# One more attention head turned through VectorE and HBM, two heads a unit sooner, and the last two down-projection units in the other order

## The chip, the cores and the metric

The kernel runs on one NeuronCore of a Trainium2 chip. TensorE (PE in the profile; PEld is its weight load) multiplies, VectorE (DVE), ScalarE (ACT) and GpSimd (POOL) do the elementwise work, and SyncE (SP) issues most of the transfers between HBM and the on-chip memory. Every engine works through its own instructions in the order in which the program issued them, and waits at an instruction until what it needs is there. The metric is the device time of one execution in microseconds (us).

## The reference

One encoder layer over 256 tokens of width 2048, in float32. Cut to what matters:

```python
h = rmsnorm(x); q, k, v, u = split(h @ w_in)        # 12 query heads, 4 key/value heads of 128
scores = q @ k.T * 128**-0.5 + alibi                # window |t - s| <= 128
m = max(scores.max(-1), sink)
p = exp(scores - m); p = p / (p.sum(-1) + exp(sink - m))
a = rmsnorm(p @ v)                                  # 1536 wide
f = rmsnorm(fourier_mix(u))                         # 512 wide
x = x + concat([a, f]) @ w_out
g, val = split(rmsnorm(x) @ w_up)                   # 5504 wide each
x = x + (gelu(conv3(g)) * val) @ w_down
y = rmsnorm(x)
```

## The kernel before

**Precision.** Each float32 operand of a product is split into a rounded part "hi" and a remainder "lo", and three products (hi by hi, hi by lo, lo by hi) are summed in PSUM. For a unit of weights, ACT writes hi (line 194, `split_high`) and DVE writes lo = raw - hi (line 202, `split_low`).

**Units.** All weights come in units of 128 x 2048 floats (1 MB; the last four are 128 x 1536). SP loads a unit into one of three `raw` buffers (line 178). The load of unit i + 3 is issued when unit i has been split, as its buffer is then free. The splits run two units ahead of the products (`step`, `ff_step`), into three buffers each of `hi` and `lo`. Units 0 to 3 make u, 4 to 7 v, 8 to 23 the four keys and twelve queries, 24 to 39 the output projection (`w_out`), and the rest the feed-forward part.

**Work beside the units.** The order of everything is written out by hand. Three tables, `before`, `beside` and `behind`, hold functions under a unit's number. `unit(i, ...)` runs `before[i]`, the unit's matmuls, `beside[i]`, the split of unit i + 2, and `behind[i]`. So what is `beside` unit i stands in the queues of ACT, DVE and SP ahead of the split of unit i + 2.

**A head's way.** The query of head h is slot s of the units (head 9 is 21, head 10 is 22, head 11 is 23), and each step is placed at a unit s + n. The scores are taken before unit s + 2 and leave PSUM beside it (`scores_out`), the exponentials run behind it (`exps`), and beside s + 3 `weigh` divides by the sums (lines 714, 717). The 256 x 256 weights must then be turned, so that the keys lie on the partitions, for the product with v (`values`, line 769). There are two ways:

- Heads 10 and 11 (not in `FLIPS`) are turned on TensorE: four 128 x 128 transposes before unit s + 4 (`turn`, line 724), split out of PSUM beside it (`turn_out`, lines 736 and 737), product before s + 5.
- Heads 0 to 9 (in `FLIPS`) are turned by the others: beside s + 3 DVE transposes 32 x 32 blocks (`flip_out`, line 327) and four transfers write them to HBM (line 330); beside s + 4 one transfer reads them back in the right order (`flip_in`, line 338); beside s + 6 they are split (`flip_parts`, lines 759 and 760); and the product stands before s + 7.

`values_out` (lines 494, 295, 296) leaves the product beside the same unit as a tile `cat`, which units 24 on multiply with `w_out`. The tile of head 10 is first read in unit 29. `total_scale` (lines 505 to 523) takes the sums of squares of the Fourier part behind unit 25.

**The end.** The last four units (`in_w_down_last`, called L0 to L3 here; i is L0's number) are multiplied twice: for the first 128 tokens (b = 0) in the order L0, L1, L2, L3, then for the others (b = 1). Each `last_product(c, b)` is nine matmuls (lines 1336 to 1338), after which DVE adds the result to the residual (line 1181), ACT squares it, and POOL multiplies it by the last norm's factors (line 1176). The splits of L0 and L1 are made two items ahead as before. Then the kernel before splits L3 (unit i + 3, `own_tiles`) into buffers of its own, and after `last_product(0, 0)` it calls `ff_step`, which runs what is left beside that item (the additions of the last `down` item, `down_out`, line 1162) and splits L2.

Of the kernel before, what the change touches and what calls it, by code (L numbers as in the profile page):

```python
# [18 lines left out]
NH = 12  # L19
# [46 lines left out]
for _g in range(NKV):  # L66
    QK_ORDER += [("k", _g)] + [("q", _g * GQA + _i) for _i in range(GQA)]

FLIPS = range(NH - 2)
QK_FIRST = {n: (2, 2) if n in (8, 12) else (1, 0) for n in range(16)}  # L70
N_U, N_V, N_QK = 0, 4, 8
N_OUT = N_QK + len(QK_ORDER)
# [25 lines left out]
def ff_items():  # L98


    def ups(first, end):
        return [(kind, j) for j in range(first, end) for kind in ("gate", "val")]

    firsts = [first for first, _ in GROUPS] + [LATE[0], NF]
    items = ups(0, firsts[1])
    for g, pattern in enumerate(PATTERNS):
        todo = {
            "u": ups(firsts[g + 1], firsts[g + 2]),
            "s": [("product", g, c, p) for c in range(2) for p in PRODUCTS[c]],
            "d": [("down", c) for c in range(4)],  # L110
        }
        items += [todo[c].pop(0) for c in pattern]
        assert not (todo["u"] or todo["s"]), (g, todo)
    return items + [("last", c) for c in range(4)]
# [3 lines left out]
def block_kernel(  # L118
# [27 lines left out]
    def f32(ap):  # L146
        return ap.bitcast(F32)

    def bank(pool, name):
        return pool.tile([P, 512], F32, tag=pool.name, name=name)  # L150
# [6 lines left out]
    items, up_index = ff_items(), {}  # L157
# [16 lines left out]
    def load(i):  # L174
        if i < len(units) and i not in raws:
            src, n = units[i]
            raws[i] = wp.tile([P, 2048], F32, tag="raw", name=f"raw{i}", bufs=RAW)
            nc.sync.dma_start(raws[i][:, 0:n], src)
# [8 lines left out]
    def split_high(i, o=0, n=2048, tiles=parts_of):  # L187

        if i >= len(units):
            return  # L190
        if i not in halves:
            tiles(i)
        s = slice(o, min(o + n, units[i][1]))
        nc.scalar.activation(halves[i][0][:, s], raws[i][:, s], AF.Copy)  # L194

    def split_low(i, o=0, n=2048, reload=True):

        if i >= len(units):
            return
        hi, lo = halves[i]  # L200
        s = slice(o, min(o + n, units[i][1]))
        nc.vector.tensor_tensor(lo[:, s], raws[i][:, s], f32(hi[:, s]), ALU.subtract)  # L202
        if s.stop == units[i][1] and reload:
            load(i + RAW)
            load_more(i + RAW)

    def split(i):

        split_high(i)
        split_low(i)  # L210
# [32 lines left out]
    def u_part(k, o, n, m=1):  # L243

        rows = ux[k // 4][:, (k < 4) * U_HEAD :].rearrange("p (k c) -> p k c", k=4)
        return rows[:, k % 4 : k % 4 + m, o : o + n]
# [22 lines left out]
    def load_more(i):  # L269

        if i == 6:
            nc.sync.dma_start(chan, c_chan)
            nc.sync.dma_start(wfs, wf)
            nc.sync.dma_start(pos, c_pos)
        if i == 7:
            nc.sync.dma_start(vec[:, 0:V_N], vecs)
            nc.sync.dma_start(rel, c_rel)
# [103 lines left out]
    before, beside, behind = {}, {}, {}  # L381

    def at(when, i, f, *a):
        when.setdefault(i, []).append((f, a))

    def run(when, i):
        for f, a in when.pop(i, []):
            f(*a)
# [13 lines left out]
    for k in range(NK):  # L402
# [3 lines left out]
        n = 1 if c < 2 else 2  # L406
# [3 lines left out]
        if q % n == 0:  # L410
            w, h = u_part(k, 0, FW, n), hi[:, q : q + n, :]
# [238 lines left out]
    def qk_out(kind, h, ps):  # L650
        tmp = ph.tile([P, S], F32, tag="tmp", name=f"tmp_{kind}{h}", bufs=2)
        nc.scalar.activation(tmp, ps[:, S : 2 * S], AF.Copy)
        add = ph.tile([P, S], F32, tag="add", name=f"add_{kind}{h}", bufs=2)
        nc.vector.tensor_tensor(add, ps[:, 0:S], tmp, ALU.add)
        if kind == "k":
            nc.vector.tensor_tensor(add, add, r1b, ALU.mult)
        st["add", kind, h] = add
# [120 lines left out]
        feature_out(st.pop(("o", h))[:, 0:S], h, vcol(V_GA + h), sq_a, h == 0)  # L778


    slot_of = {kh: N_QK + n for n, kh in enumerate(QK_ORDER)}
    for i in range(N_QK, N_OUT + 8):
        heads = {i - s: h for (kind, h), s in slot_of.items() if kind == "q"}
        new = [kh for kh, s in slot_of.items() if i - s == 1]
        for n, h in sorted(heads.items()):
            if n == 5 + 2 * (h in FLIPS):
                at(before, i, values, h)
        if 4 in heads and heads[4] not in FLIPS:
            at(before, i, turn, heads[4])
        if 2 in heads:  # L790
            at(before, i, scores, heads[2])
        for kind, h in new:
            at(beside, i, lambda k=kind, h=h: qk_out(k, h, st.pop(("ps", k, h))))
        if 6 in heads and heads[6] in FLIPS:
            at(beside, i, flip_parts, heads[6])
        for kind, h in new:
            at(beside, i, qk_parts, kind, h)
        for n, h in sorted(heads.items()):
            if n == 5 + 2 * (h in FLIPS):
                at(beside, i, values_out, h)  # L800
        if 3 in heads:
            at(beside, i, weigh, heads[3])
            if heads[3] in FLIPS:
                at(beside, i, flip_out, heads[3])
        if 4 in heads:
            at(beside, i, flip_in if heads[4] in FLIPS else turn_out, heads[4])
        if 2 in heads:
            at(beside, i, scores_out, heads[2])
        if 2 in heads:
            at(behind, i, exps, heads[2])  # L810
# [68 lines left out]
    for n, (c, kq) in enumerate(OUT_ORDER):  # L879
        i = N_OUT + n  # L880
# [14 lines left out]
        if kq >= 2:  # L895
            part = "a" if kq == 2 else "f"
            ps = ps_a[c] if kq < 3 else ps_a[c, "f"]
            last = c in added
# [171 lines left out]
    def split_item(n):  # L1070
        if n >= len(items):
            return
        it = items[n]
        if n in up_index:
            split(up_index[n])
            if pending:
                pending.pop(0)()
        else:
            while pending:
                pending.pop(0)()  # L1080
            split_product(*it[1:])

    def ff_step(n):
        run(beside, n)
        split_item(n + 2)
        run(behind, n)
# [91 lines left out]
    def last_post(c, b, ps, o=0, n=512):  # L1178

        xb = xs[c][:, b, o : o + n]  # L1180
        nc.vector.tensor_tensor(xb, ps, xb, ALU.add)
        if o + n < 512 or c < 3:
            k = c if c < 3 else 4
            junk = wp.tile([P, 512], F32, tag="junk", name=f"junkc{c}{b}")
            nc.scalar.activation(
                junk[:, 0:n], xb, AF.Square, scale=D**-0.5, accum_out=ssq3[:, b, k : k + 1]
            )
# [58 lines left out]
    for q in range(OPEN):  # L1246
# [6 lines left out]
        if q == 1:  # L1253
            i = up_index[3]
# [71 lines left out]
    i = up_index[n]  # L1326


    def last_product(c, b, o=0, n=512):
        hi, lo = halves[i + c]  # L1330
        ps = bank(dn, f"ps_e{c}{b}{o}")[:, 0:n]
        for q, k in enumerate(LAST):
            w = slice(q * 512 + o, q * 512 + o + n)
            ah, al = (act[k][:, p * S + b * P : p * S + (b + 1) * P] for p in range(2))
            end = q == len(LAST) - 1
            nc.tensor.matmul(ps, ah, hi[:, w], start=q == 0, stop=False)
            nc.tensor.matmul(ps, al, hi[:, w], start=False, stop=False)
            nc.tensor.matmul(ps, ah, lo[:, w], start=False, stop=end)
        if (c, b) == (0, 0):
            ff_step(items.index(("last", 0)))  # L1340
        last_post(c, b, ps, o, n)

    split_high(i + 3, tiles=own_tiles)
    split_low(i + 3)
    last_product(0, 0)
    first_squares(0)
    by_factors(0, 0, engine=nc.gpsimd)
    for c in (1, 2):
        last_product(c, 0)
        by_factors(c, 0, engine=nc.gpsimd)  # L1350
    last_product(3, 0)
    v = add_squares(0, 0, 512, ssq3[:, 0, 3:4], 4)
    r3 = last_scale(0, other_squares(0, v))
# [128 lines left out]
```

## Time and profile before

| | us |
|---|---|
| median of 3 runs (lowest, highest) | 936.0 (935.55, 936.22) |
| the profiled execution | 935.62 |
| its span, first to last instruction | 933.8 |
| PE busy in the span | 924.0 |
| DVE, ACT, POOL busy | 772.0, 541.9, 62.0 |

The heads 9 to 11 run beside the units 24 to 28, which lie between 155 and 188 us of the span. The first matmul of the last products starts at 908.46 us, the last one at 925.55 us. What follows that is the tail: squares, the last scale, and the transfers out.

How to read it: an answer in order of time has the start in us, the duration in us, the engine, the line of the kernel, the operation, what it writes and what it reads, how many were merged, and in square brackets the idle time of the engine before it and what ended that. Matmuls are pipelined, so each row of PE lasts longer than its distance to the next row's start; that distance (the pitch) is what a matmul costs when nothing waits.

### The profile page before, as it was taken

What the parts mean: (1) busy time and instruction counts of PE and PEld (TensorE: products, weight loads), DVE (VectorE), ACT (ScalarE), POOL (GpSimd) and SP (SyncE); (2) the same over time, 40 slices, a digit from 0 to 9 for tenths busy, and PEclk for the clock granted to TensorE, in tenths of its full rate; (3) what the DMA queues carried; (4) which work ended last, traced back from release to release, by engine and by line L of the source; (5) the groups of instructions that cost most, each with busy time, mean ns of one, the idle gap of its engine ahead of it and who ended that gap; (6) DMA issues with size and microseconds to landing.
All of it is one profiled execution on the core that took longest, in us unless ns stands there. A gap on an engine that the chain in (4) does not pass through costs nothing.

```text
span 933.8 us, 12856 instructions
## 1 busy us (share of the span) xinstructions
PE 924.0 (99%) x4985; PEld 800.2 (86%) x4985; DVE 772.0 (83%) x986; ACT 541.9 (58%) x674; POOL 62.0 (7%) x80
## 2 busy tenths in 40 slices
PE   9999999999999999999999999999999999999996
PEld 7888998888888888888888888888888888888885
DVE  7668988787768877898877997879978789989986
ACT  7756767546455655565555665555655556655553
POOL 0101111200000000000000000000000000000002
PEclk9999999999999999999999999999999999999998
DMA  9965777467677668787798779887787968879652
GB/s 368 312 226 166 241 238 217 175 195 276 223 277 252 202 206 259 241 277 258 232 300 248 246 210 297 221 260 231 274 237 247 299 216 270 248 241 271 188 181 90
DMA packets 57949, 224.44 MB, mean 240 GB/s; under 512 B 23296, under 2 KB 28544, under 8 KB 34336
## 3 DMA queue, kind: packets, MB, share of 16 engines
q1 hardware_dynamic: 53200, 193.86, 57.9%
q0 software_dynamic: 4544, 29.49, 17.1%
q8 instruction: 39, 0.64, 0.3%
q10 hardware_dynamic: 144, 0.26, 0.1%
q14 instruction: 22, 0.18, 0.1%
HBM read 216.78 MB, written 6.82 MB: 239 GB/s over the span
## 4 chain that ended last, share of the span: by engine, by line
PE 96%; DVE 2%; DMA 1%; ACT 1%; issue 1%; POOLq 0%; POOL 0%; ACTq 0%; DVEq 0%
PE ps_val L363 25%; PE ps_gate L363 25%; PE ps_q L363 7%; PE ps_P L1155 3%; PE ps_P L1156 3%; PE ps_P L1157 3%; PE ps_N L1155 3%; PE ps_N L1156 3%; PE ps_N L1157 3%; PE ps_a L348 2%; PE ps_a L346 2%; PE ps_k L363 2%; PE ps_a L347 2%; PE ps_s L675 1%; PE ps_o L769 1%; DVE lo L202 1%
## 5 line engine op out<-in xcount | busy, mean ns | idle before, releaser
L202 DVE TENSOR_TENSOR lo<-raw,hi 128x2048 fp32r<-128x2048 f32 (+2 forms) x133 | 295.1, 2220 | 34.7 <-ACT hi L194 34.3
L194 ACT ACTIVATE hi<-raw 128x2048 fp32r<-128x2048 f32 (+1 forms) x131 | 246.9, 1887 | 29.8 <-PE ps_a L347 11.3
L363 PE MATMUL ps_gate<-hU,hi 128*128 128x512 f32 x688 | 236.1, 389 | 0.0
L363 PE MATMUL ps_val<-hU,hi 128*128 128x512 f32 x688 | 236.1, 389 | 0.0
L363 PE MATMUL ps_gate<-hU,lo 128*128 128x256 f32 x688 | 189.9, 276 | 0.0
L363 PE MATMUL ps_val<-hU,lo 128*128 128x256 f32 x687 | 189.6, 276 | 0.0
L363 PEld LDWEIGHTS ps_val<-hU,hi 128*128 128x128 f32 x688 | 129.1, 188 | 26.9
L363 PEld LDWEIGHTS ps_gate<-hU,hi 128*128 128x128 f32 x688 | 129.1, 188 | 26.8
L363 PEld LDWEIGHTS ps_gate<-hU,lo 128*128 128x128 f32 x688 | 129.1, 188 | 1.3
L363 PEld LDWEIGHTS ps_val<-hU,lo 128*128 128x128 f32 x687 | 128.9, 188 | 1.3
L936 ACT ACTIVATE ft_g<-ps_gate 128x256 f32<-128x256 f32 x43 | 16.5, 384 | 120.6 <-PE ps_gate L363 120.6
L936 ACT ACTIVATE ft_v<-ps_val 128x256 f32<-128x256 f32 x43 | 16.4, 383 | 86.8 <-PE ps_val L363 86.8
L363 PE MATMUL ps_q<-hT,hi 128*128 128x512 f32 x192 | 65.0, 391 | 0.0
L1155 PE MATMUL ps_P<-hi_P,op_P 128*128 128x512 f32 x144 | 56.0, 389 | 0.0
L1156 PE MATMUL ps_P<-hi_P,op_P 128*128 128x512 f32 x144 | 56.0, 389 | 0.0
L1157 PE MATMUL ps_P<-lo_P,op_P 128*128 128x512 f32 x144 | 56.0, 389 | 0.0
L363 PE MATMUL ps_q<-hT,lo 128*128 128x256 f32 x192 | 51.2, 277 | 0.0
L1053 DVE TENSOR_TENSOR lo_N<-sumw,hi_N 128x2048 fp32r<-128x2048 f32 (+1 forms) x20 | 41.5, 2077 | 9.4 <-ACT hi_N L1052 9.2
L1155 PE MATMUL ps_N<-hi_N,op_N 128*128 128x512 f32 x108 | 42.0, 389 | 0.0
L1156 PE MATMUL ps_N<-hi_N,op_N 128*128 128x512 f32 x108 | 42.0, 389 | 0.0
L1157 PE MATMUL ps_N<-lo_N,op_N 128*128 128x512 f32 x108 | 42.0, 389 | 0.0
L363 PEld LDWEIGHTS ps_q<-hT,hi 128*128 128x128 f32 x192 | 35.2, 188 | 6.6
(402 smaller groups left out, 1587.1 us busy)
## 6 DMA issues: line engine op xcount, KB each, us to landing
raw<-in_w_up SPq DMA_DIRECT2D x86, 1024.0 KB, 6.7
raw<-in_w_in SPq DMA_DIRECT2D x20, 1024.0 KB, 5.8
raw<-in_w_out SPq DMA_DIRECT2D x16, 1024.0 KB, 4.8
sumw<-in_w_down POOLq DMA_DIRECT2D x16, 1024.0 KB, 8.6
raw<-in_w_down_late SPq DMA_DIRECT2D x4, 1024.0 KB, 6.9
raw<-in_w_down_last SPq DMA_DIRECT2D x4, 768.0 KB, 4.2
turnp<-flip SPq DMA_DIRECT2D x40, 64.0 KB, 2.2
flop<-turnp SPq DMA_DIRECT2D x10, 256.0 KB, 3.5
```

Of the source, the lines that this page charges most:

```text
L194: nc.scalar.activation(halves[i][0][:, s], raws[i][:, s], AF.Copy)
L202: nc.vector.tensor_tensor(lo[:, s], raws[i][:, s], f32(hi[:, s]), ALU.subtract)
L346: nc.tensor.matmul(ps, ah, wh, start=first and q == q0, stop=False)
L347: nc.tensor.matmul(ps, al, wh, start=False, stop=False)
L348: nc.tensor.matmul(ps, ah, wl, start=False, stop=last and q == q0 + len(kk) - 1)
L363: nc.tensor.matmul(ps[:, x], (hi, lo)[i][:, k * P : (k + 1) * P], hk(k)[:, x], start=n == 0 and k == 0, stop=n == len(order) - 1 and k == ...
L675: nc.tensor.matmul(ps[:, b * S : (b + 1) * S], qT[:, qo + b * P : qo + (b + 1) * P], kT[:, ko : ko + S], start=n == 0, stop=n == 2,)
L936: nc.scalar.activation(tmp, ps[:, S : 2 * S], AF.Copy)
L1053: nc.vector.tensor_tensor(lo, src, f32(hi), ALU.subtract)
L1155: nc.tensor.matmul(ps, o[:, 0, p, :], hi[:, s], start=first and p == 0, stop=False)
L1156: nc.tensor.matmul(ps, o[:, 1, p, :], hi[:, s], start=False, stop=False)
L1157: nc.tensor.matmul(ps, o[:, 0, p, :], lo[:, s], start=False, stop=last and p == n - 1)
```

## The change

Head 10 joins `FLIPS`, so that head 11 alone is turned on TensorE. Heads 9 and 10 are `SOON`: their split and their product stand one unit sooner than for the other flipped heads, at s + 5 and s + 6. For head 9 this is beside unit 26 and before unit 27 (it was 27 and 28). For head 10 it is beside 27 and before 28 (its turn was before 26, and its product before 27). At the end, L2 (i + 2) is split into the buffers of its own ahead of `last_product(0, 0)`, and L3 (i + 3) after it into the common ring, behind the additions of the last `down` item.

```diff
-FLIPS = range(NH - 2)
+FLIPS = range(NH - 1)
+SOON = (NH - 3, NH - 2)
...
+    def values_at(h):
+        return 5 + 2 * (h in FLIPS) - (h in SOON)
+
...
-            if n == 5 + 2 * (h in FLIPS):
+            if n == values_at(h):
                 at(before, i, values, h)
...
-        if 6 in heads and heads[6] in FLIPS:
-            at(beside, i, flip_parts, heads[6])
+        for n, h in sorted(heads.items()):
+            if n == values_at(h) - 1 and h in FLIPS:
+                at(beside, i, flip_parts, h)
...
-            if n == 5 + 2 * (h in FLIPS):
+            if n == values_at(h):
                 at(beside, i, values_out, h)
...
         if (c, b) == (0, 0):
-            ff_step(items.index(("last", 0)))
+            n0 = items.index(("last", 0))
+            run(beside, n0)
+            split(i + 3)
+            run(behind, n0)
         last_post(c, b, ps, o, n)
 
-    split_high(i + 3, tiles=own_tiles)
-    split_low(i + 3)
+    split_high(i + 2, tiles=own_tiles)
+    split_low(i + 2)
     last_product(0, 0)
```

## The prediction

> **What bounds the kernel now.** I read the page first, then PE's waits, then the two places that the diff touches, engine by engine in order of time. The page's rows of busy time and of the chain that ended last:
>
> ```profile
> PE 924.0 (99%) x4985; PEld 800.2 (86%) x4985; DVE 772.0 (83%) x986; ACT 541.9 (58%) x674; POOL 62.0 (7%) x80
> PE 96%; DVE 2%; DMA 1%; ACT 1%; issue 1%; POOLq 0%; POOL 0%; ACTq 0%; DVEq 0%
> ```
>
> In the second row the reader sees that 96% of the chain is TensorE, which the first row has busy for nearly the whole span. So the time can fall only where PE gets fewer instructions, where a wait of PE goes, or in the tail. PE's waits (waited for, us in total, times, longest) show one outside the first units:
>
> ```profile
> PE ps_e L1338 <- DVE lo L202: 0.5, 1, 0.5
> PE ps_u L420 <- ACT hT L295: 0.3, 1, 0.3
> ```
>
> The change touches both kinds: four transposes of PE, and that wait on `lo` in the last products.
>
> **Head 10's transposes go.** PE in order of time about unit 26 (the transposes of head 10 at 168.05) and at the start of unit 27 (the product of head 10, then the transposes of head 11), and the group of all eight transposes (min/median/max ns):
>
> ```profile
> 168.05 0.60 PE L724 MATMUL ps_t<-ident,sc 128*128 128x128 f32 x4
> 168.41 0.48 PE L346 MATMUL ps_a<-hi,cat 128*128 128x512 f32 x1
> 168.72 0.40 PE L347 MATMUL ps_a<-hi,cat 128*128 128x512 f32 x1
> ...
> 174.00 0.40 PE L769 MATMUL ps_o<-pt,v_hi 128*128 128x256 f32 x2
> ...
> 174.71 0.60 PE L724 MATMUL ps_t<-ident,sc 128*128 128x128 f32 x4
> ```
>
> ```profile
> L724 PE MATMUL ps_t<-ident,sc x8: 272/273/276, 168.1 to 175.0; 128*128 128x128 f32 x8
> ```
>
> And PE in the last products, about its wait:
>
> ```profile
> 912.54 0.39 PE L1336 MATMUL ps_e<-hi,act 128*128 128x512 f32 x1
> 912.76 0.39 PE L1337 MATMUL ps_e<-hi,act 128*128 128x512 f32 x1
> 913.64 0.50 PE L1338 MATMUL ps_e<-lo,act 128*128 128x512 f32 x1 [0.49 <-DVE lo L202]
> 913.98 0.40 PE L1336 MATMUL ps_e<-hi,act 128*128 128x512 f32 x1
> ```
>
> The pitch of a 512-wide matmul that waits for nothing is 912.76 - 912.54 = 0.22 by rounded starts; I use 0.23. From the first transpose to the second matmul after it pass 168.72 - 168.05 = 0.67 us. Without transposes it would be one pitch, so they cost 0.67 - 0.23 = **0.44**. Two other values are possible. If the slow first matmul (0.31 to the next) belongs to the change of product and not to the transposes, the gain is 168.41 - 168.05 = 0.36. If each transpose costs its whole duration, it is 4 x 0.273 = 1.09. I take 0.44, as starts on one engine in a stretch without waits leave no room for more; 0.36 and 1.09 stay as ends.
>
> The Trainium skill (TensorE: Matmul & The Clock Gate, Part 4: PE-mode transpose) has about 275 ns for a 128 x 128 transpose in a kernel's context, for bf16, most of it access latency. The row's 273 ns agrees as a duration, but the pitch within this trace is a third of it; by the page's figure as a cost the four would give 1.10 us (an estimate from the page).
>
> The products move without cost: head 9's six matmuls go from unit 28 to 27, head 10's from 27 to 28. PE has as many of them, and each unit as many as before.
>
> **What replaces the transposes.** On ACT and DVE the split from PSUM (lines 736, 737) becomes one in two halves from SBUF, and DVE gets one more block transpose. DVE in order of time, units 24 to 26, and the groups of the flipped tile with the landing of its loads (us, min/median/max):
>
> ```profile
> 156.97 0.71 DVE L327 STREAM_TRANSPOSE flip<-sc 128x512 f32<-128x512 f32 x1
> ...
> 163.28 0.48 DVE L691 CUSTOM_DVE_ANT_0 sc<-ps_s,rel,sink 128x256 f32<-128x256 f32 x1
> ...
> 170.15 1.22 DVE L523 COPY rstdf<-sums_f 32x2 f32<-32x2 f32 x4 [1.79 <-POOL sums_f L519]
> 171.38 0.48 DVE L296 SCALAR_TENSOR_TENSOR cat<-ps_o,vec,cat 128x256 fp32r<-128x256 f32 x1
> 171.78 0.16 DVE L714 RECIPROCAL ex<-sm 128x2 f32<-128x2 f32 x1
> 171.97 0.62 DVE L717 TENSOR_SCALAR sc<-sc,ex 128x256 f32<-128x256 f32 x2
> ```
>
> ```profile
> L760 DVE TENSOR_TENSOR pt<-flop,pt x20: 414/418/973, 97.1 to 175.6; 128x256 fp32r<-128x256 f32 x20
> ...
> DMA to landing us min/median/max: 2.7/3.5/6.4
> ```
>
> Head 10's transpose comes ahead of the row at 163.28 and moves all later work of DVE by 0.71, so the row at 171.38 (head 8's `cat`) could start at 172.09. There now stands head 9's split, moved up one unit: 2 x 0.42 = 0.84, or 0.42 + 0.97 = 1.39 if one half is as slow as the slowest row. It ends at 172.93 (173.48). PE wants it for head 9's product at 174.00 - 0.36 to 0.44, some 173.6: in time by both. Then come head 8's `cat` and head 11's `weigh`, which took 171.97 + 0.62 - 171.38 = 1.21: done at 174.14 (174.69). The transposes of head 11 want that at 174.71 - 0.44 = 174.27. So the spare is 0.13, or PE waits 0.42. This is the tightest place of the change. I take no wait, as 0.42 is the median of twenty halves; 0.42 of waiting stays as an end. `turn_out` of head 10 (line 737) leaves DVE ahead of the split of unit 28, so the work behind is late by about a split less that, and those units are wanted a unit and more later: nothing.
>
> **SP's queue.** SP in order of time: head 9's four writes, the load of unit 29, head 9's read.
>
> ```profile
> 157.71 1.83 SPq L330 DMA_DIRECT2D turnp<-flip  x4
> 160.90 0.35 SPq L178 DMA_DIRECT2D raw<-in_w_out  x1
> 161.93 0.38 SPq L338 DMA_DIRECT2D flop<-turnp  x1
> ```
>
> Five transfers are added. Head 10's writes stand in the queue ahead of head 9's read and wait for the transpose: 163.28 + 0.71 = 163.99. With 1.83 to issue they end at 165.8, and head 9's read moves from 161.93 to about 165.9. It lands after 2.7 to 6.4, median 3.5: at 169.4 (168.6 to 172.3). ACT then needs two halves before DVE can finish, but DVE isn't free before 172.09, so up to a landing near 171 nothing is lost. At 172.3 head 11's `weigh` follows some 0.5 later than worked out, and PE waits up to 0.8. The load of unit 30 behind it waits for DVE's split of unit 27, some 0.71 later, and is used units later. Head 10's read comes when its writes have landed (head 9's were read at 161.93, which is 2.4 after the end of their issues at 157.71 + 1.83 = 159.54), 168.2, and even 6.4 later it is 174.6, ahead of its split beside unit 27 and its product at some 180. Nothing on either.
>
> **The end: L2 before L3.** ACT, then DVE in order of time; then the loads of L1 and L2 (first and last issue, and landing):
>
> ```profile
> 907.44 2.86 ACT L194 ACTIVATE hi<-raw 128x1536 fp32r<-128x1536 f32 x2 [2.96 <-DMA raw<-in_w_down_last]
> ```
>
> ```profile
> 904.51 1.76 DVE L202 TENSOR_TENSOR lo<-raw,hi 128x1536 fp32r<-128x1536 f32 x1 [0.61 <-ACT hi L194]
> 908.97 1.76 DVE L202 TENSOR_TENSOR lo<-raw,hi 128x1536 fp32r<-128x1536 f32 x1 [2.69 <-ACT hi L194]
> 910.64 1.28 DVE L1162 TENSOR_TENSOR xs<-ps_l,xs 128x512 f32<-128x512 f32 x2
> 911.84 1.75 DVE L202 TENSOR_TENSOR lo<-raw,hi 128x1536 fp32r<-128x1536 f32 x1
> ...
> 925.87 0.42 DVE L1181 TENSOR_TENSOR xs<-ps_e,xs 128x256 f32<-128x256 f32 x1 [0.40 <-PE ps_e L1338]
> ```
>
> ```profile
> L178 SPq DMA_DIRECT2D raw<-in_w_down_last x2: 328/328/328, 895.8 to 898.4; - x2
> ...
> DMA to landing us min/median/max: 4.1/4.2/4.2
> ```
>
> This is the wait: ACT stands 2.96 for the load of L3 though L2 has lain there since 898.4 + 4.2 = 902.6. DVE then splits L3 (908.97), does the additions (910.64), and ends L2's `lo` at 913.59; PE has wanted it a pitch after 912.76. After the change L2's `hi` starts when ACT has done L1's (904.5) and takes 2.86 / 2 = 1.43; its `lo` ends near 906.27 + 1.76 = 908.0, 4.5 ahead of need. Gain: 913.98 - 912.76 = 1.22 for two pitches of 0.23, so **0.76**. The row with PE's wait alone gives 0.5, the lower end.
>
> Next in line is L3. Its load has landed by 907.44, where ACT's wait ended, and the ring buffer is free when the last `down` product ends, just after the last products' start. The additions take DVE 1.28 from there (say 908.7 to 910.0), ACT's `hi` runs beside them, and `lo` ends by 911.8. PE comes to L3 after L2's nine matmuls, 912.54 + 9 x 0.23 - 0.44 = 914.2: 2.4 to spare. The tail follows its matmuls: the last addition (925.87) waits for PE, so it moves with PE.
>
> **Sum.** 0.44 + 0.76 = 1.20 off the profiled execution's 935.62: 934.4. That execution stands 0.4 below the median of the runs, 936.0, to which I apply the same: **934.8**, that is 0.13% less. About 0.2% (1.9 us) is what a measurement of this kernel can tell from no change, so my forecast is: the same, on the fast side.
>
> **Rivals.** (1) Slower: head 9's weights come too late, as SP issues head 10's writes first and the read then lands behind them. If the read took its longest, 6.4, only after the writes had landed (2.4), it would come at 165.9 + 8.8 = 174.7. ACT's two halves, DVE's two, `cat` and `weigh` follow: 0.4 + 0.84 + 1.21, and head 11's turn starts at 177.2 and not 174.27: PE waits 2.9. That makes 936.0 - 1.2 + 2.9 = 937.7. It is slower than before from a landing at 173.0 on, 7.1 after the issue, and by more than 0.2% from 174.9 on. Against it: none of the reads in the trace took more than 6.4. (2) The mild form: the read toward its longest, or the slow half: 0.3 to 0.8 of waiting, 935.1 to 935.6. For it speaks the spare of 0.13. (3) Faster by 0.2%: the transposes cost 0.273 each: 1.09 + 0.76 = 1.85, so 934.1, at the edge. Against it: the start at 168.41. (4) The change at the end only moves the wait, to L3: 936.0 - 0.44 = 935.6. Against it: 2.4 to spare.
>
> **How the numbers follow.** My forecast 0.58; (2) 0.20; (3) 0.08, most of it past the bound; (4) 0.04; (1) 0.10, most of it past the bound, since a read that comes so late has no upper end in these rows. So faster 0.07, same 0.85, slower 0.08. The forecast's own range is 934.4 to 935.4: the ends 0.36 and 0.5 give 0.86 instead of 1.20, and the runs spread by some 0.3. For 8 in 10: down to (3)'s 934.1 less 0.1, and up through (2) and (4) to 935.6 and the runs' spread and a second thing of (2)'s size, 936.4.
>
> **What would show it.** Right: no PE wait at line 1338; four rows at line 724 and not eight; unit 26's first matmul right behind head 8's product; the last products beginning 0.44 earlier and the last matmul 1.2. Wrong: a wait of PE at line 769 or 724 near 174 (on `pt` or `sc`), with a read at line 338 that landed after 171; a wait at line 1336 or 1338 for L3's `hi` or `lo`. It would also be wrong if the stretch between, which nothing touches, took another time: its units are fed by the same queues.

## The result

The changed kernel takes 934.57 us (median of 21 runs, 934.04 to 935.96), the kernel before 935.88 (21 runs on the same chips): a ratio of 0.9987, with a 95% interval of 0.9981 to 0.9993. The forecast was 934.8 and 0.13% less. The profiled execution of the changed kernel has 934.68 us and a span of 932.9. Behind the numbers of the experiments stand three runs of 951 to 952 us (one with head 11 flipped too, two of the kernel before), some 15 above all others of their kernel; the medians and ratios leave them out.

PE's waits in the changed kernel (waited for, us in total, times, longest):

```profile
PE ps_warm L289 <- POOL ones L281: 1.0, 1, 1.0
PE ps_u L421 <- ACT hT L296: 0.2, 1, 0.2
```

The wait on `lo` in the last products is gone, and none has come in its place. PE about unit 26, and at the start of unit 27, where the transposes of head 11 are the only ones left:

```profile
168.53 0.28 PE L770 MATMUL ps_o<-pt,v_lo 128*128 128x256 f32 x1
168.65 0.40 PE L347 MATMUL ps_a<-hi,cat 128*128 128x512 f32 x1
168.88 0.40 PE L348 MATMUL ps_a<-hi,cat 128*128 128x512 f32 x1
...
174.73 0.28 PE L770 MATMUL ps_o<-pt,v_lo 128*128 128x256 f32 x1
174.85 0.60 PE L725 MATMUL ps_t<-ident,sc 128*128 128x128 f32 x4
175.21 0.48 PE L347 MATMUL ps_a<-hi,cat 128*128 128x512 f32 x1
```

Unit 26 begins one narrow pitch (0.12) behind head 8's product, and its second matmul follows at 0.23 and not at 0.31: both parts of the 0.44 were the transposes'. At 174.85 head 11's transposes follow head 9's product at the usual pitch, so nothing waited there. DVE shows why that was close (units 25 and 26):

```profile
171.47 1.22 DVE L524 COPY rstdf<-sums_f 32x2 f32<-32x2 f32 x4 [1.79 <-POOL sums_f L520]
172.73 0.76 DVE L761 TENSOR_TENSOR pt<-flop,pt 128x256 fp32r<-128x256 f32 x2
173.41 0.48 DVE L297 SCALAR_TENSOR_TENSOR cat<-ps_o,vec,cat 128x256 fp32r<-128x256 f32 x1
173.80 0.15 DVE L715 RECIPROCAL ex<-sm 128x2 f32<-128x2 f32 x1
173.99 0.62 DVE L718 TENSOR_SCALAR sc<-sc,ex 128x256 f32<-128x256 f32 x2
```

By the last row head 11's weights are done at 174.61, 0.24 ahead of 174.85; the run with a second transpose, below, puts what there was to spare at 0.36. Head 9's read, now behind head 10's writes on SP:

```profile
L339 SPq DMA_DIRECT2D flop<-turnp x1: 399/399/399, 166.7 to 166.7; - x1
...
DMA to landing us min/median/max: 2.8/2.8/2.8
```

It has landed by 169.5, 3 us before DVE is free for it.

The profiled executions of these kernels start differently, by up to 1.2 us in the first units. The comparison by stretches leaves that out: each row is from the start of one first matmul to the start of the next, read from PE in order of time.

| stretch, us | before | changed | difference |
|---|---|---|---|
| start to the first output product (unit 24) | 154.94 | 155.53 | +0.59 |
| that to the first product of unit 28 | 27.14 | 26.69 | -0.45 |
| that to the first up product | 65.33 | 65.33 | 0.00 |
| that to the first of the last products | 661.05 | 661.05 | 0.00 |
| that to the last matmul | 17.09 | 16.31 | -0.78 |
| that to the end | 8.27 | 7.99 | -0.28 |

Two of the three gains were in the prediction with these sizes (0.44 and 0.76). The third, in the tail, was not. The first row is not of the change: over the profiles below it goes from 154.9 to 156.1. In these two profiles most of it lies in the first matmuls of u, where from the first start to the fifth pass 1.11 us before and 1.86 in the changed kernel.

ACT and DVE at the end of the changed kernel:

```profile
903.13 2.87 ACT L195 ACTIVATE hi<-raw 128x1536 fp32r<-128x1536 f32 x2 [3.90 <-PE ps_l L348]
908.57 1.49 ACT L195 ACTIVATE hi<-raw 128x1536 fp32r<-128x1536 f32 x1 [2.57 <-PE ps_l L348]
```

```profile
904.66 3.43 DVE L203 TENSOR_TENSOR lo<-raw,hi 128x1536 fp32r<-128x1536 f32 x2 [0.61 <-ACT hi L195]
908.00 1.49 DVE L1167 TENSOR_TENSOR xs<-ps_l,xs 128x512 f32<-128x512 f32 x2
910.10 1.76 DVE L203 TENSOR_TENSOR lo<-raw,hi 128x1536 fp32r<-128x1536 f32 x1 [0.61 <-ACT hi L195]
```

L1 and L2 are split back to back, done at 908.1, and L3 at 911.9. ACT no longer waits for a load, but for PE to leave the ring buffer.

### The profile page after: what moved, and what is told of

Its sections match the earlier page's. It is cut to its first block, busy times and chain, and to the rows that moved or that the text cites. A ratio compares the mean times of both kernels' runs of the same rounds, so it can differ in the third digit from the quotient of the medians.

```text
span 932.9 us, 12860 instructions
## 1 busy us (share of the span) xinstructions
PE 924.0 (99%) x4981; PEld 800.8 (86%) x4981; DVE 772.4 (83%) x988; ACT 542.3 (58%) x675; POOL 63.0 (7%) x80
## 3 DMA queue, kind: packets, MB, share of 16 engines
q0 software_dynamic: 4544, 29.49, 17.1%
## 4 chain that ended last, share of the span: by engine, by line
PE 98%; DMA 0%; ACT 0%; DVE 0%; issue 0%; POOLq 0%; POOL 0%; ACTq 0%
PE ps_val L364 25%; PE ps_gate L364 25%; PE ps_q L364 7%; PE ps_P L1161 3%; PE ps_P L1160 3%; PE ps_P L1162 3%; PE ps_N L1160 3%; PE ps_N L1161 3%; PE ps_N L1162 3%; PE ps_a L347 2%; PE ps_k L364 2%; PE ps_a L349 2%; PE ps_a L348 2%; PE ps_s L676 1%; PE ps_o L770 1%; PE ps_ff L347 1%
```

## The experiments

All ratios are to the kernel before on the same chip. Their intervals are about 0.0009 to either side, which is 0.8 us: the measured time alone can't tell parts of 0.3 us apart, so the verdicts on the parts rest on the stretches, and the measured time is given beside them. The changed kernel itself was run beside the last group alone.

**The order of the last units alone.** Heads as before:

```diff
-FLIPS = range(NH - 1)
-SOON = (NH - 3, NH - 2)
+FLIPS = range(NH - 2)
+SOON = ()
```

> The order of the last two units alone; heads 9 and 10 as before. Theory (two gains that add: the transposes' pitch on TensorE, 0.44 us, and the wait on lo in the last products, 0.76 us): 0.76 less than before, a ratio of 0.9992, no wait of PE at the lo matmul of the last products, eight transposes on PE. Rival (the whole gain is the wait's, transposes cost TensorE nothing): 1.2 less, a ratio of 0.9987, the same as the whole change.

Measured: 935.30 against 935.59, a ratio of 0.9998 (0.9989 to 1.0006). The stretches: unit 24 to 28 27.14, last products 16.31, tail 8.38. So the parts add as the theory has them, and the rival falls by the stretches. The measured time shows 0.3 where 0.76 was expected; the interval holds both.

**The heads alone.** The last units in the order of before:

```diff
-            n0 = items.index(("last", 0))
-            run(beside, n0)
-            split(i + 3)
-            run(behind, n0)
+            ff_step(items.index(("last", 0)))
...
-    split_high(i + 2, tiles=own_tiles)
-    split_low(i + 2)
+    split_high(i + 3, tiles=own_tiles)
+    split_low(i + 3)
```

> Heads 9 and 10 as in the change; the last two units in the order of before. Theory: 0.44 less than before, a ratio of 0.9995; the PE wait on lo in the last products stays at 0.5 by the profile. Rival (whole gain is the wait's): as before, a ratio of 1.000. Rival (a transpose costs its whole duration of 0.27): 1.1 less, a ratio of 0.9988.

Measured: 934.42 against 935.59, 0.9990 (0.9982 to 0.9999). Unit 24 to 28 took 26.69, which is the 0.45 again; that stretch, and not the measured time, tells against a transpose costing its whole duration, as 0.9990 lies nearer to that rival's 0.9988 than to 0.9995 and the interval holds both. But two things were not as expected: the last products took 16.32, with no wait, and the tail 7.99 and not 8.27. ACT at the end of this kernel:

```profile
906.54 1.49 ACT L195 ACTIVATE hi<-raw 128x1536 fp32r<-128x1536 f32 x1 [2.17 <-DMA raw<-in_w_down_last]
908.31 1.50 ACT L195 ACTIVATE hi<-raw 128x1536 fp32r<-128x1536 f32 x1 [0.28 <-PE ps_l L348]
```

It waits for L3's load in the same way, but the load landed 4.1 after its issue, where it took 4.9 in the profile of before. The landing of L3's load, first in the kernel before, then here:

```profile
DMA to landing us min/median/max: 4.9/4.9/4.9
```

```profile
DMA to landing us min/median/max: 4.1/4.1/4.1
```

With 4.1, L2's `lo` is ready just when PE asks for it. So the 0.76 is no constant: it is what the load takes beyond about 4.1 (the expectations below say 4.15).

**VectorE a transpose later.** The changed kernel, head 10's block transpose done twice:

```diff
-        nc.vector.transpose(t, src)
+        for _ in range(2 if name == "p10" else 1):
+            nc.vector.transpose(t, src)
```

> The changed kernel, with VectorE's block transpose of head 10 done twice (the same result written twice), which delays all that VectorE does after it by another 0.64 to 0.71. Theory (VectorE's order sets when head 11's weights are ready; in the changed kernel they were ready 0.24 to 0.33 before TensorE wanted them): TensorE now waits 0.3 to 0.5 at the transposes of head 11, for sc, and the time is 0.3 to 0.5 above the changed kernel's, a ratio of 0.9991 to before. Rival (the read of head 9 from HBM sets it): no wait, the time of the changed kernel, 0.9987, since that read lands no later.

Measured: 935.14, 0.9996 (0.9987 to 1.0005), 0.5 above the changed kernel's 934.6. PE, then the end of head 11's `weigh` on DVE:

```profile
174.71 0.28 PE L771 MATMUL ps_o<-pt,v_lo 128*128 128x256 f32 x1
175.21 0.72 PE L726 MATMUL ps_t<-ident,sc 128*128 128x128 f32 x4 [0.23 <-DVE sc L719]
```

```profile
174.71 0.62 DVE L719 TENSOR_SCALAR sc<-sc,ex 128x256 f32<-128x256 f32 x2
```

The transposes of head 11 start 0.50 behind the matmul ahead of them and not 0.12, and the stretch from unit 24 to 28 grows by 0.49. Counted from unit 24's first matmul (155.51 here, 155.53 in the changed kernel), DVE's row ends at 19.82 where the changed kernel has 19.08. So 0.74 of delay on DVE cost 0.38 at this place and another 0.11 in the slower start behind it, and DVE had 0.36 to spare in the changed kernel. That is the theory; the read from HBM was no part of it.

**Head 9's read later.** The changed kernel, that read issued behind the load of unit 30:

```diff
-            at(beside, i, flip_in if heads[4] in FLIPS else turn_out, heads[4])
+            at(behind if heads[4] == 9 else beside, i, flip_in if heads[4] in FLIPS else turn_out, heads[4])
```

> The changed kernel, with the read of head 9 issued behind the load of unit 30 on SyncE's queue (it stood ahead of it, right behind head 10's writes). It is then issued near 168.4 beside that 1 MB load and lands after 4.5 to 6.4, at 172.9 to 174.8 in place of 169.4. Theory (there are 1.5 to 2.5 us of spare up to there, then each later us costs one): TensorE waits 0.5 to 2.4 in all, at head 9's product (pt) and at the transposes of head 11 (sc); the time is 0.5 to 2.4 above the changed kernel's, a ratio of 0.9992 to 1.0013. Rival (VectorE alone sets it, as it is busy with the Fourier sums until 172.7): within 0.2 of the changed kernel.

Measured: 935.85, 1.0002 (0.9993 to 1.0011), some 1.3 above the changed kernel. SP, and PE where it waits:

```profile
168.16 0.35 SPq L179 DMA_DIRECT2D raw<-in_w_out  x1
168.62 0.92 SPq L339 DMA_DIRECT2D flop<-turnp  x2
```

```profile
174.36 0.78 PE L770 MATMUL ps_o<-pt,v_hi 128*128 128x256 f32 x2
174.97 0.28 PE L770 MATMUL ps_o<-pt,v_lo 128*128 128x256 f32 x1
175.09 0.40 PE L770 MATMUL ps_o<-pt,v_hi 128*128 128x256 f32 x2
175.33 0.28 PE L770 MATMUL ps_o<-pt,v_lo 128*128 128x256 f32 x1
176.30 0.72 PE L725 MATMUL ps_t<-ident,sc 128*128 128x128 f32 x4 [0.69 <-DVE sc L718]
```

Both heads' reads went out together, each took 5.2 to 5.3, and ACT began head 9's split at 173.81, where the changed kernel has 169.48. PE lost at both places, 1.32 in the stretch. So the read's landing is a second deadline, at some 172.4 in the changed kernel (174.85 less the 2.45 that the prediction has for ACT and DVE behind it), and that kernel was early enough by 3 us. One late landing bears the price out: this run's unit 24 starts 0.23 later, so its 173.8 is 1.2 past the deadline, and it cost 1.32, of which 0.12 is the slower start behind the wait. By the start of the kernel before the landing is at 173.0, where the prediction's rival (1) has the time of before, and the ratio is 1.0002: that rival had its mechanism and its price right. What didn't come in the change is a landing that late.

**Five transfers more, nothing else.** This asks where the tail's 0.28 comes from. The kernel before, with `rel` loaded in six pieces:

```diff
-            nc.sync.dma_start(rel, c_rel)
+            for a, b in ((0, 96), (96, 176), (176, 256), (256, 336), (336, 416), (416, 512)):
+                nc.sync.dma_start(rel[:, a:b], c_rel[:, a:b])
```

> The kernel before, with the load of the distances (rel) in six pieces and not one: five more transfers issued by SyncE early on, the same bytes, nothing else. Theory (the changed heads add five transfers to SyncE's instructions, and by that alone move a pause of about 0.3 us that SyncE makes ahead of the last output transfer in the kernel before): the tail after the start of the last matmul falls from 8.3 to 8.0 us, the time by 0.3, a ratio of 0.9997. Rival (the shorter tail has to do with the heads themselves or is chance): the tail stays at 8.3, a ratio of 1.000.

Measured: 935.81 against 935.88, 0.9998 (0.9989 to 1.0007); the tail is 7.99. SP's last two transfers, first in the kernel before, then here, then in the changed kernel:

```profile
928.89 0.38 SPq L1218 DMA_DIRECT2D out_y<-z_P  x1
929.68 0.33 SPq L1218 DMA_DIRECT2D out_y<-xs  x1
```

```profile
929.81 0.40 SPq L1219 DMA_DIRECT2D out_y<-z_P  x1
930.30 0.41 SPq L1219 DMA_DIRECT2D out_y<-xs  x1
```

```profile
928.24 0.40 SPq L1223 DMA_DIRECT2D out_y<-z_P  x1
928.73 0.40 SPq L1223 DMA_DIRECT2D out_y<-xs  x1
```

The last transfer comes 0.79 after the one ahead of it in the kernel before, and 0.49 in the other two. The profiles with before's number of transfers have the pause just there (before, the end alone, and before again, below), those with five more don't have it. In the old order with L3 loaded twice (next), which has one transfer more, it stands one transfer sooner: 0.79 between the issues at 935.87 and 936.66. So this gain of the change has nothing to do with heads: more instructions in SP's stream move a pause of 0.3. (It is not all that moves the tail: with ten more, in the last two versions below, the pause is gone too, and the tail is 8.15 and 8.17.) What SP does in the pause the trace doesn't name, so its cause stays open. In the measured time the gain is not to be seen (0.1 of 0.3, well inside the interval). The last products took 17.05 here, with a landing of 4.8 for L3.

**L3 loaded twice,** in the old order and in the new. It lands some 9 us after the first issue:

```diff
-            nc.sync.dma_start(raws[i][:, 0:n], src)
+            for _ in range(2 if i == len(units) - 1 else 1):
+                nc.sync.dma_start(raws[i][:, 0:n], src)
```

> The kernel before, with the last unit (L3) loaded twice into the same buffer, one after the other, so that it lands about 4.2 later. Theory (in the old order ScalarE and VectorE wait for L3's load before they split L2, and TensorE waits for L2): TensorE's wait in the last products grows to about 4 us, the last products take about 20.5 and not 17.1, the time is 3.5 above before, a ratio of 1.0037. Rival (L3's load has nothing to do with it): as before.

> The changed kernel, with L3 loaded twice in the same way. Theory (with L2 first, L3 has 2.4 to spare after its split, which begins a microsecond after the landing): the spare takes in nearly all of the 4.2; TensorE waits 0 to 0.6 for L3, the last products take 16.3 to 16.9, a ratio of 0.9987 to 0.9994. Rival (the change moves the wait from L2 to L3): a wait of 2 or more, a ratio above 1.001.

Measured in the old order: 942.29 against 935.88, 1.0069 (1.0055 to 1.0082); in the new: 935.57, 0.9997 (0.9987 to 1.0006). The old order waits for L3 before it splits L2, as the theory says, and the new one takes the delay in its spare: the last products took 16.35. But both times were missed. In the new order the lateness came out behind the products: the tail is 8.95 and not 7.99, as DVE does the first additions behind L3's split (the first at 915.20, where the changed kernel has 911.77) and never catches up. And in the old order the last products took 23.34 where 20.5 was expected, 7.0 above the 16.31 without a wait:

```profile
915.87 0.50 PE L1337 MATMUL ps_e<-hi,act 128*128 128x512 f32 x1 [1.96 <-ACT hi L195]
916.21 0.39 PE L1338 MATMUL ps_e<-hi,act 128*128 128x512 f32 x1
919.15 0.80 PE L1339 MATMUL ps_e<-lo,act 128*128 128x512 f32 x1 [2.55 <-DVE lo L203]
919.75 0.63 PE L1337 MATMUL ps_e<-hi,act 128*128 128x512 f32 x1
```

By stretches of the same kernel (us, busy time of PE, PEld, DVE, ACT and POOL, granted clock, DMA):

```profile
916.25:916.50 0.25, 0.25 (x2) 0.00 (x0) 0.25 (x1) 0.00 (x0) 0.00 (x0) 1.00 0.00 0
916.50:916.75 0.25, 0.10 (x1) 0.00 (x0) 0.25 (x1) 0.00 (x0) 0.00 (x0) 0.53 0.00 0
...
919.00:920.00 1.00, 0.85 (x2) 0.75 (x3) 0.70 (x2) 0.27 (x1) 0.00 (x0) 0.50 0.00 0
...
923.50:924.00 0.50, 0.50 (x4) 0.41 (x3) 0.00 (x0) 0.50 (x2) 0.00 (x0) 1.00 0.00 0
```

There are two waits, 1.96 and 2.55, two matmuls apart. The granted clock falls to 0.50 at about 916.5, behind the first wait, while the second of those matmuls runs and before the second wait begins (916.60), and matmuls then come every 0.43 and not 0.23 until 923.2. Of the 7.0, some 4.9 are the waits and 2.1 the slow clock behind them. The 4.9 is close to what the load had over the 4.1: it landed 9.2 after its first issue, 5.1 beyond. In all four executions of this kernel the mean granted clock is 0.994 to 0.996, where those of the other kernels have 0.997 to 0.999, so the fall was no accident of the profiled one.

**A step further: head 11 flipped too.** For this the output units (1, 3) and (0, 2) change places, so that head 11's `cat` is first read a unit later:

```diff
-FLIPS = range(NH - 1)
-SOON = (NH - 3, NH - 2)
+FLIPS = range(NH)
+SOON = (NH - 3, NH - 2, NH - 1)
...
-OUT_ORDER = [(0, 0), (1, 0), (0, 1), (1, 1), (0, 3), (0, 2), (1, 3), (1, 2)]
+OUT_ORDER = [(0, 0), (1, 0), (0, 1), (1, 1), (0, 3), (1, 3), (0, 2), (1, 2)]
...
-            at(behind if (c, kq) == (0, 2) else beside, i + 1, out_add, c, part, ps)
+            if (c, kq) == (0, 3):
+                out_add(c, part, ps)
+            else:
+                at(behind if (c, kq) == (0, 2) else beside, i + 1, out_add, c, part, ps)
...
-                at(beside, i + 2, flip_x_in, c)
-                at(beside, i + 4, flip_x_parts, c)
+                at(beside, i + 2 + (c == 1), flip_x_in, c)
+                at(beside, i + 4 + (c == 1), flip_x_parts, c)
```

> A step further than the change: head 11 is flipped too, with its split beside unit 28 and its product before 29. For that, the output units (1, 3) and (0, 2) change places, so that cat 8 to 11 is first read in unit 30; the additions of (0, 3) come right behind unit 28, and the second flip of x one unit later. Theory: no transposes on PE, another 0.44 off the changed kernel, the stretch from the first output product to the first up product goes from 92.02 to 91.57, a ratio of 0.9982. Rival (head 11's way through HBM is too late, as its exponentials come last): a wait of TensorE for pt or cat of 0.5 to 3, a ratio of 0.9990 to 1.002.

Measured: 935.19 against 935.88, 0.9993 (0.9984 to 1.0002). The stretch from unit 24 to the first up product took 92.38, where the changed kernel has 92.02 and 91.57 was expected: 0.8 too much, of which some 0.7 was lost at head 10's product. ACT shows the wait:

```profile
180.25 0.73 ACT L760 ACTIVATE pt<-flop 128x256 fp32r<-128x256 f32 x2 [7.58 <-DMA flop<-turnp]
```

Head 10's read was issued at 177.37, as it stood behind head 11's writes on SP, which wait for DVE. It is not head 11 that came late, as the rival had it, but head 10 behind it.

**The read ahead of the writes.**

```diff
+            if heads[3] == 11:
+                at(beside, i, flip_in, heads[4])
             if heads[3] in FLIPS:
                 at(beside, i, flip_out, heads[3])
-        if 4 in heads:
+        if 4 in heads and heads[4] != 10:
```

> The run with all heads flipped, with one order changed: head 10's read stands in SyncE's queue ahead of head 11's writes, and so no longer waits for VectorE's transpose of head 11. Theory (in that run SyncE's order held head 10's read back to 177.4, and TensorE waited for it): the read is issued near 168.5 as in the changed kernel, the wait of TensorE goes, the stretch from the first output product to the first up product falls from 92.38 to 91.57, and the time is 0.45 below the changed kernel's, a ratio of 0.9982 to 0.9985. Rival (ScalarE's or VectorE's order is what held it): the stretch stays above 92.2, a ratio of 0.999.

Measured: 934.91 against 935.80, 0.9990 (0.9981 to 0.9999). The read went out at 167.94, and PE no longer waits for it. But the stretch took 92.14, not 91.57. PE, and DVE at the same time:

```profile
203.00 0.39 PE L349 MATMUL ps_a<-lo,cat 128*128 128x512 f32 x1
203.54 0.47 PE L347 MATMUL ps_a<-hi,cat 128*128 128x512 f32 x1
```

```profile
202.65 1.40 DVE L836 SCALAR_TENSOR_TENSOR xs<-ps_a,rstda,xs 128x512 f32<-128x512 f32 x2
```

By the order of the rows, PE stands still at the first product of a new column block until DVE has added the first half of the old one, whose PSUM it takes over: a product that was moved a unit on has its addition a unit later. This place has 0.39 of the missing 0.57. In the run with all heads flipped, where PE comes to the same product later, the addition ended at 204.18 and PE passed at 204.45 without a stop, which fits; no run was made that takes the stop away, so it is read from the rows and not shown. The version is no better than the change: 934.91 beside 934.61.

**The changed kernel and the kernel before once more,** on the chip of the last run, as they are.

> The changed kernel as it is, on the same chip as the other two, to set them beside it. Theory (0.45 for the transposes, 0.3 for SyncE's pause in the tail, and for the order of the last units what L3's load has over 4.15, some 0.26 as a mean over the landings of the profiles so far): 1.0 below before, a ratio of 0.9989. If the wait on lo came in every run of the kernel before with its 0.76: 1.5 below, 0.9984.

> The kernel before as it is, for another profile of its end. Theory (TensorE's wait in the last products is what L3's load takes beyond 4.15, and not a fixed 0.76): the last products take 16.3 plus that excess; the tail is 8.3, with SyncE's pause. Rival: 17.1 whatever the landing.

Measured: the changed kernel 934.61, 0.9986 (0.9977 to 0.9995); the kernel before 935.72, 0.9998 of itself. The first interval holds both 0.9989 and 0.9984, so the measured time doesn't say whether the wait came in every run. The profile of before has a landing of 4.5 for L3:

```profile
L178 SPq DMA_DIRECT2D raw<-in_w_down_last x1: 328/328/328, 902.8 to 902.8; - x1
...
DMA to landing us min/median/max: 4.5/4.5/4.5
```

Its last products took 16.70, and its tail 8.37. So the four profiles in the old order have landings of 4.1, 4.5, 4.8 and 4.9, and last products of 16.32, 16.70, 17.05 and 17.09, against 16.31 in the new order. Beyond 4.1 the wait is the landing's excess, to 0.02, and the rival of a fixed 17.1 falls. The seven profiles in the new order with one load of L3 have landings of 4.0 to 4.6, and 16.31 in each: there the landing no longer matters.

## Why the prediction was right

**The transposes: right, with the size.** 0.44 was forecast; 0.45 is in the stretch of the changed kernel and of the heads alone, and not in that of the end alone. The pitch was the price, not the duration of 0.273, and rival (3) falls with that. The figure of the Trainium skill (TensorE: Matmul & The Clock Gate, Part 4: PE-mode transpose), about 275 ns, agrees with the trace as a duration and not as a cost.

**What replaces them: right, and the tightest place was the right one.** The spare was put at 0.13; the end of DVE's row leaves 0.24, and the run with VectorE a transpose later gives 0.36. The two halves took 0.76 together where 0.84 was added up, as rows that follow each other on DVE overlap. That run shows that this place pays when DVE is later, and PE waits at no other place behind it. Rival (2), a wait of 0.3 to 0.8 here, did not come in the changed kernel.

**SP's queue: right.** The read moved from 161.93 to 166.66 (0.6 of that is the later start) and landed in 2.8, where 3.5 was taken. Rival (1) was a real mechanism, since in the run with all heads flipped the same queue did hold a read back, and in the run with the late read PE paid what that rival's sum gives; in the change the read had 3 us to spare.

**The end: the mechanism right, the size taken from one execution.** PE waited for L2 because ACT waited for L3, and with L2 first it waits for neither. But the term of 0.76 was read from a profile with a slow load. Over the four profiles of the old order the last products are 0.78, 0.39, 0.74 and 0.01 above 16.31, a mean of 0.48. The step that failed is "The row with PE's wait alone gives 0.5, the lower end": the lower end was nothing, as a landing of 4.1 (which the quoted row has for another load of this kind) would have shown when put into the same sum. Rival (4) falls: L3 was split by 911.9, and its first matmul in the changed kernel starts at 914.72.

**The tail: wrong.** "It moves with PE" held for the additions, not for SP's last transfer, which came 0.3 sooner because of five more transfers in SP's stream, which the forecast counted as queue time at their own place alone.

**The sum was right by luck, as two errors offset each other:** the parts are 0.45, 0.48 as a mean of four, and 0.28 to 0.39 in the tail (8.27, 8.37 and 8.38 with the pause, 7.99 without), so 1.21 to 1.32, where 0.44 + 0.76 = 1.20 was forecast. The measured time has 1.31 (0.7 to 1.8), and 1.19 in the second comparison. It fell within 0.2%, as forecast.

## What to carry to other kernels

In a kernel whose TensorE is never idle, a change is worth the pitches that it takes off TensorE and the waits of TensorE that it ends, if every new deadline (on the vector engine, on the transfer queue) is worked out and has some tenths to spare. The pitches could be told to 0.01 us here (0.44 and 0.45). A wait that hangs on a load differs with each execution's landing, so it wants the landing put in at both ends of those that the trace shows, not at the one profile's. And when a piece of work is moved a step on, ask what its buffer held up: the all-flipped version lost its gain first to a queue and then, by the order of the rows, to the later release of PSUM.

## What was not expected of the hardware

- One wait of TensorE of 1.96 us, and two matmuls behind it, were followed by a fall of the granted clock to 0.50. It lasted through the next wait of 2.55 and some four microseconds of work behind that: waits of 4.9 cost 7.0. The Trainium skill (TensorE: Matmul & The Clock Gate, Why this matters for your kernels) warns of idle gaps above about 3 us; here the gap ahead of the fall was shorter.
- SyncE paused by 0.3 us ahead of the last output transfer in the kernel before, and five more transfers, issued some 900 us earlier, took that away.
- The same 768 KB load, beside the same work, landed after 4.1 to 4.9 us in one execution or another, and the first units differ by 1.2 us between executions, while every stretch in which TensorE waits for nothing repeats to 0.01 us.
